# Both products of an MLP as 2x2 block products with seven multiplications, on one Trainium2 core

## The chip, the core and the metric

The kernel runs on one core of one Trainium2 chip. The engines of a core work side by side, each through its own list of instructions in a fixed order: PE (TensorE) multiplies matrices, PEld is its weight load, DVE (VectorE), ACT (ScalarE) and POOL (GpSimd) work element by element, and SP (SyncE) issues the transfers between DRAM and the core's memory. The metric is the device time of one execution in microseconds (us), median of several runs.

## The reference

The program is a stack of three mixing layers of width 1024 over 1024 tokens. The change touches only its end: the norm before the last MLP, the MLP, and the norm behind it. In float32:

```python
    merged = ...                                   # sum of four gated branches, (1, 1024, 1024)
    x = x + rms_norm(merged @ w_out, norm_mix_post)

    h2 = rms_norm(x, norm_mlp_pre)
    u = jax.nn.relu(h2 @ w_mlp_in)                 # w_mlp_in (1024, 4096)
    x = x + rms_norm((u * u) @ w_mlp_out, norm_mlp_post)   # w_mlp_out (4096, 1024)
    return x
```

## The kernel before, in words

Activations lie transposed: a page is 128 features by 512 tokens, so an activation of width 1024 is 8 feature blocks times 2 token halves, 16 pages. A float32 operand is held as two pages or weight tiles, a high part (rounded to the multiplier's format) and a low part (the rest), made by `split` (L101): ACT casts the high part (L104), DVE subtracts it from the source (L105). A product of one weight block of 128x128 with one page is three matmuls of 128x512 in `mm3` (L111): high by high (L113), high by low (L114), low by high (L115).

`merge` (L1755) multiplies the branches by their gates and by `w_out` (`proj`) and ends with `norms`, once for each token half: a row norm (`rnorm`, with small matmuls at L198 and L206 and a power on POOL at L141), the old x from DRAM added (L1803, L1804), x stored to DRAM as `x3`, and a second norm whose 8 results are split into pages `H`.

`mlp` (L1825) then goes over the 4096 inner features in 8 chunks of 4 blocks. `hidden` takes each block: `wload` (L144) fetches 512 KB of weights into `raw` (two buffers) and splits them into `whi` and `wlo` (128x1024), 8 feature blocks by three matmuls give one page per token half, ACT copies it (L1840), DVE applies relu and square in one instruction (L1841), and `split` makes pages `M`. `project` multiplies the 4 blocks of the chunk with the matching rows of `w_mlp_out` for the 8 output blocks and adds the result to 16 accumulators `Y` (L1862). In the first and the last chunk the token halves go one after the other, otherwise together. `finish` is the last norm, for one half under the products of the other.

Counted: each of the two MLP products has 32 x 8 blocks x 2 halves x 3 = 1536 matmuls of 128x512, 3072 in all.

The order of each engine's instructions is set when the program is built, by a scheduler that moves instructions within their data dependences and the free buffers. A tile of a pool can be taken again only when the last reader of its former content is done.

Of the kernel before, what the change touches and what calls it, by code (L numbers as in the profile page):

```python
# [11 lines left out]
F32 = mybir.dt.float32  # L12
F32R = mybir.dt.float32r
BF16 = mybir.dt.bfloat16
AF = mybir.ActivationFunctionType
ALU = mybir.AluOpType
AX = mybir.AxisListType

S = 1024
D = 1024  # L20
P = 128
# [4 lines left out]
N_RAW, N_HI = 2, 2  # L26
NEARLY, NLATE = 4, 8
NS, NL, NN = 32, 7, 5


class Kern:
# [1723 lines left out]
    def merge(self, br):  # L1755
# [41 lines left out]
        def norms(half, ys, acc):  # L1797
            hs = slice(half * 512, half * 512 + 512)
            r = self.rnorm(acc, 1.0 / 1024.0)
            for f in range(8):  # L1800
                xo = self.T("xo", 2)
                nc.sync.dma_start(out=xo, in_=self.x2[f * P:(f + 1) * P, hs])
                nc.vector.scalar_tensor_tensor(out=ys[f], in0=ys[f], scalar=self.n2[:, 8 + f:9 + f], in1=r, op0=ALU.mult, op1=ALU.mult)  # L1803
                nc.vector.tensor_tensor(out=ys[f], in0=ys[f], in1=xo, op=ALU.add)  # L1804
                nc.sync.dma_start(out=self.x3[f * P:(f + 1) * P, hs], in_=ys[f])
            res.append(self.norm_half(ys, self.n2[:, 16:24]))
# [12 lines left out]
        norms(0, ys[0], accs[0])  # L1819
        for f in range(8):  # L1820
            proj(f, 1, ys[1], accs[1])
        norms(1, ys[1], accs[1])
        return self.pair_halves(res)

    def mlp(self, H, out):  # L1825


        nc = self.nc
        FC = 4
        last = 32 // FC - 1  # L1830
        Y = [[None, None] for _ in range(8)]
        def hidden(ch, halves, between=()):
            U = [[None, None] for _ in range(FC)]
            for j in range(FC):
                w = self.wload(self.seg("w_mlp_in", (ch * FC + j) * 1024, 8, 128), 8, 128)
                for half in halves:
                    pt = self.ps("mm")
                    self.fm(pt, w, H, half)
                    t = self.T("M", 32)
                    nc.scalar.copy(t, pt)  # L1840
                    nc.vector.scalar_tensor_tensor(out=t, in0=t, scalar=0.0, in1=t, op0=ALU.max, op1=ALU.mult)  # L1841
                    hi, lo = self.T("M", 32, F32R), self.T("M", 32, F32R)
                    self.split(hi, lo, t)
                    U[j][half] = (hi, lo)
                if between:
                    between[j]()
            return U

        def project(ch, U, halves):
            for dp in range(4):  # L1850
                w = self.wload(self.seg("w_mlp_out", (ch * 4 + dp) * 1024, 4, 256), 4, 256)
                for dd in range(2):
                    d = 2 * dp + dd
                    wd = [(a[:, dd * P:(dd + 1) * P], b[:, dd * P:(dd + 1) * P]) for a, b in w]
                    for half in halves:
                        pt = self.ps("mm")
                        self.fm(pt, wd, U, half)
                        if ch == 0:
                            Y[d][half] = self.T("Y", 16)
                            nc.scalar.copy(Y[d][half], pt)  # L1860
                        else:
                            nc.vector.tensor_tensor(out=Y[d][half], in0=Y[d][half], in1=pt, op=ALU.add)  # L1862

        def olds(half):
            X = [self.T("M", 32) for _ in range(8)]
            for d in range(8):
                nc.sync.dma_start(out=X[d], in_=self.x3[d * P:(d + 1) * P, half * 512:half * 512 + 512])
            return X

        def finish(half, X):  # L1870

            hs = slice(half * 512, half * 512 + 512)
            acc = self.T("yacc", 2)
            for d in range(8):
                self.sumsq_add(acc, Y[d][half], d == 0)
            r = self.rnorm(acc, 1.0 / 1024.0)

            def scale(d0):
                for d in (d0, d0 + 1):
                    y = Y[d][half]  # L1880
                    nc.vector.scalar_tensor_tensor(out=y, in0=y, scalar=self.n2[:, 24 + d:25 + d], in1=r, op0=ALU.mult, op1=ALU.mult)
                    nc.vector.tensor_tensor(out=y, in0=y, in1=X[d], op=ALU.add)
                    nc.sync.dma_start(out=out[d * P:(d + 1) * P, hs], in_=y)
            return [lambda d=d: scale(d) for d in range(0, 8, 2)]

        for ch in range(last):
            for halves in ((0,), (1,)) if ch == 0 else ((0, 1),):
                project(ch, hidden(ch, halves), halves)
        project(last, hidden(last, (0,)), (0,))
        U = hidden(last, (1,), finish(0, olds(0)))  # L1890
        X = olds(1)
        project(last, U, (1,))
        for fn in finish(1, X):
            fn()

    def second_block(self, H, out, end_banks):
# [4 lines left out]
        with tc.tile_pool(name="gp", bufs=1, reuse_waits="tile") as self.gp:  # L1901
# [21 lines left out]
            end_banks()  # L1923
            with self.banks("tail", 4, 0, 1, 2), self.phase("tail"):
                H2 = self.merge(brd)
                self.mlp(H2, out)

# [198 lines left out]
```

## Time and profile before

| | |
|---|---|
| median of 3 runs | 3508.95 us (3502.64 to 3509.22) |
| profiled execution, own time | 3508.32 us |
| its span, first to last instruction | 3506.5 us |
| mean granted TensorE clock in it | 0.984 of full speed |
| PE busy | 3369.9 us (96% of the span) |
| DVE, ACT, POOL busy | 1966.9, 1321.3, 109.2 us |

The profile is one execution. Its span runs from the first to the last instruction; 1.8 us of the measured time lie around it. The part that the change touches is the end of the span, from about 2700 us on: the two `norms` lie between 2720 and 2810 us, the products of the MLP follow, the last of them ends at 3486 us, and the last norm closes the span. A busy time counts an engine as busy while an instruction of it runs. Matmuls overlap one another in the pipeline, so the cost of one is the distance between the starts of two, not its own duration.

### The profile page before, as it was taken

To read this page: it belongs to the slowest core of one execution; us is meant where nothing else is said; L and a number is where in the kernel's file an instruction comes from. 1 tells how busy PE (TensorE), PEld (TensorE's weight loads), DVE (VectorE), ACT (ScalarE), POOL (GpSimd) and SP (SyncE) were. 2 spreads that over 40 slices of the span, in tenths; PEclk is the share of its full clock that TensorE was granted. 3 is DMA by queue.
4 is the path that set the end of the run, shared out by engine and by line. 5 is a ranking of instruction groups with operands and counts; after the bars stand their busy time and mean duration, and the time that the engine had idled before them with its cause. 6 is when DMAs were issued, how large, how long until landed. Compare 5 with 4: busy or idle time off the path is not lost.

```text
span 3506.5 us, 45207 instructions
## 1 busy us (share of the span) xinstructions
PE 3369.9 (96%) x18181; PEld 2812.7 (80%) x18181; DVE 1966.9 (56%) x3418; ACT 1321.3 (38%) x2106; POOL 109.2 (3%) x132
## 2 busy tenths in 40 slices
PE   7999999999999999999999999999989899999997
PEld 5888988777888888787777777779768788888886
DVE  6767644556767644565664367453477743333336
ACT  4656412334655312443312345463233442222222
POOL 0000000000000000000100000000000000000000
PEclk9999999999999999999999999999999999999998
DMA  5111111452111111443231211122275421111114
GB/s 185 57 36 51 50 55 57 140 179 86 48 43 36 41 46 63 158 162 119 87 95 65 67 55 56 49 70 75 85 256 178 158 89 48 48 49 49 49 61 149
DMA packets 138707, 302.34 MB, mean 86 GB/s; under 512 B 23944, under 2 KB 41336, under 8 KB 137984
## 3 DMA queue, kind: packets, MB, share of 16 engines
q1 hardware_dynamic: 129280, 282.65, 24.7%
q10 hardware_dynamic: 9216, 16.78, 1.3%
q8 instruction: 143, 2.34, 0.3%
q14 instruction: 68, 0.56, 0.1%
HBM read 245.30 MB, written 58.28 MB: 87 GB/s over the span
## 4 chain that ended last, share of the span: by engine, by line
PE 83%; DVE 5%; issue 5%; ACT 3%; DMA 3%; POOL 1%; SPq 0%; DVEq 0%; POOLq 0%; ACTq 0%
PE mm L113 21%; PE mm L114 21%; PE mm L115 21%; PE lg L388 2%; PE lg L389 2%; PE tp L512 2%; PE pv L113 1%; PE pv L206 1%; PE pv L114 1%; PE pv L115 1%; DMA S<-mix 1%; PE tp L198 1%; DVE wlo L105 1%; PE tp L1392 1%; ACT whi L104 1%
## 5 line engine op out<-in xcount | busy, mean ns | idle before, releaser
L113 PE MATMUL mm<-H,whi 128*128 128x512 f32 x2400 | 958.2, 400 | 26.9 <-DVE S L369 5.0
L115 PE MATMUL mm<-H,wlo 128*128 128x512 f32 x2400 | 949.4, 396 | 5.9 <-DVE wlo L105 5.7
L114 PE MATMUL mm<-H,whi 128*128 128x512 f32 x2400 | 949.8, 396 | 2.1 <-DVE H L105 2.1
L104 ACT CAST whi<-raw 128x1024 fp32r<-128x1024 f32 (+1 forms) x340 | 334.4, 984 | 860.3 <-PE mm L114 768.7
L105 DVE TENSOR_TENSOR wlo<-raw,whi 128x1024 fp32r<-128x1024 f32 (+1 forms) x340 | 387.4, 1140 | 421.6 <-ACT whi L104 409.9
L113 PEld LDWEIGHTS mm<-H,whi 128*128 128x128 f32 x2400 | 456.5, 190 | 125.5 <-ACT H L107 7.2
L115 PEld LDWEIGHTS mm<-H,wlo 128*128 128x128 f32 x2400 | 455.7, 190 | 104.2 <-DVE wlo L105 12.3
L114 PEld LDWEIGHTS mm<-H,whi 128*128 128x128 f32 x2400 | 456.2, 190 | 92.7 <-DVE H L105 2.9
L113 PE MATMUL mm<-whi,H 128*128 128x256 f32 x960 | 277.2, 289 | 3.9 <-DVE S L576 3.2
L114 PE MATMUL mm<-wlo,H 128*128 128x256 f32 x960 | 274.6, 286 | 3.1 <-DVE wlo L105 3.1
L115 PE MATMUL mm<-whi,H 128*128 128x256 f32 x960 | 273.7, 285 | 0.0
L113 PE MATMUL mm<-M,whi 128*128 128x512 f32 x640 | 249.5, 391 | 1.7 <-ACT whi L104 1.5
L115 PE MATMUL mm<-M,wlo 128*128 128x512 f32 x640 | 249.7, 390 | 0.2 <-DVE wlo L105 0.2
L114 PE MATMUL mm<-M,whi 128*128 128x512 f32 x640 | 249.5, 390 | 0.0
L113 PEld LDWEIGHTS mm<-whi,H 128*128 128x128 f32 x960 | 184.6, 192 | 6.8 <-issue 4.2
L114 PEld LDWEIGHTS mm<-wlo,H 128*128 128x128 f32 x960 | 184.8, 193 | 5.1 <-DVE wlo L105 4.2
L115 PEld LDWEIGHTS mm<-whi,H 128*128 128x128 f32 x960 | 184.6, 192 | 0.4
L489 DVE CUSTOM_DVE_ANT_0 lg<-lg,strip 128x1024 f32<-128x1024 f32 x128 | 155.2, 1234 | 25.8 <-PE lg L389 25.6
L1862 DVE TENSOR_TENSOR Y<-Y,mm 128x512 f32<-128x512 f32 x112 | 77.0, 687 | 159.1 <-PE mm L115 159.0
L493 ACT ACTIVATE L<-lg,mx 128x1024 f32<-128x1024 f32 x128 | 142.7, 1118 | 36.5 <-DVE mx L489 30.3
L113 PEld LDWEIGHTS mm<-M,whi 128*128 128x128 f32 x640 | 120.2, 188 | 28.0 <-ACT whi L104 1.9
L115 PEld LDWEIGHTS mm<-M,wlo 128*128 128x128 f32 x640 | 120.5, 188 | 25.6 <-DVE wlo L105 0.6
(455 smaller groups left out, 4968.0 us busy)
## 6 DMA issues: line engine op xcount, KB each, us to landing
raw<-in_w_in SPq DMA_DIRECT2D x106, 512.0 KB, 3.6
raw<-in_w_out SPq DMA_DIRECT2D x48, 512.0 KB, 4.0
raw<-in_w_gate SPq DMA_DIRECT2D x46, 512.0 KB, 3.5
raw<-in_w_mlp_in SPq DMA_DIRECT2D x40, 512.0 KB, 3.3
raw<-in_w_mlp_out SPq DMA_DIRECT2D x40, 512.0 KB, 3.2
Y<-gates SPq DMA_DIRECT2D x64, 256.0 KB, 5.0
gates<-gs ACTq DMA_DIRECT2D x60, 256.0 KB, 2.0
mix<-S SPq DMA_DIRECT2D x48, 256.0 KB, 2.1
```

Of the source, the lines that this page charges most:

```text
L104: nc.scalar.copy(hi, src)
L105: nc.vector.tensor_tensor(out=lo, in0=src, in1=hi.bitcast(F32), op=ALU.subtract)
L113: mm(out, lh, rh, start=start, stop=False)
L114: mm(out, lh, rl, start=False, stop=False)
L115: mm(out, ll, rh, start=False, stop=stop)
L198: self.nc.tensor.matmul(ss[:, n * i + j:n * i + j + 1], acc[:, j * P:(j + 1) * P], self.one, start=True, stop=True)
L388: mm(out, Q[m][qb // 4][:, sl], KH[m][half][:, o:o + kn], start=True, stop=False)
L389: mm(out, Q[m][qb // 4][:, sl], KL[m][half][:, o:o + kn], start=False, stop=not more)
L489: nc.vector.tensor_tensor_reduce(out=lg, in0=lg, in1=strip[:, w0:w0 + 1024], op0=ALU.add, op1=ALU.min, scale=-1.0, scalar=3.0e38, accum_ou ...
L493: nc.scalar.activation(pm, lg, AF.Exp, bias=mx, scale=-1.0, accum_out=sm)
L512: nc.tensor.transpose(tp[:, j, :], pm[:, kb * P:(kb + 1) * P], self.ident)
L1862: nc.vector.tensor_tensor(out=Y[d][half], in0=Y[d][half], in1=pt, op=ALU.add)
```

## The change

Both MLP products are computed as products of 2x2 blocks with seven block products in place of eight. For one pair of output blocks (2g, 2g+1) the weights are A11, A12 (block 2g, first and second half of the contraction) and A21, A22 (block 2g+1); the activations are B11, B21 (token half 0, first and second half of the contraction) and B12, B22 (token half 1). With

- S1 = A21+A22, S2 = S1-A11, S3 = A11-A21, S4 = A12-S2 (sums of weights, `side_weights`),
- T1 = B12-B11, T2 = B22-T1, T3 = B22-B12, T4 = T2-B21 (sums of pages, `side_sums`),

the seven products are A11 B11, A12 B21, S2 T2, S1 T1, S3 T3, A22 T4 and S4 B22; DVE adds them up to the four results. All the sums S and T are made by POOL. Each S and each T is split into a high and a low part like any operand before.

First product: `norms` now leaves seven sets of four split pages (`keep`) in place of `H`, and its steps for token half 1 are dealt out between the first products. For g = 0 to 7 the two products A11 B11 and A12 B21, which need only half 0, are done ahead in a loop of their own (E = 8); then for g = 0 to 15 the others (five for g below 8, seven from 8 on). After relu and square, the four results of the group go through `side_sums` again, and all seven pages (B11, B21, T2, T1, T3, T4, B22) are written to DRAM.

Second product: the 16 groups of inner pages are contracted in chunks of 3, 3, 3, 3 and 4. For each chunk the seven sets are loaded from DRAM and split (`load`), and four pairs of output blocks are done with seven products of 9 (in the last chunk 12) matmuls. POOL adds three of the intermediate results to the accumulators `Y` (`gather`), DVE the others. In the last chunk half 0 is finished first; S1 T1 and S4 B22, which only half 1 needs, follow in a loop of their own with the weights loaded and summed again, next to the last norm of half 0.

The memory pool of the branch stage is closed before the end stage, which takes 52 tiles of 128x512 that all its pages share.

```diff
+NT = 52
+CHUNKS = [range(0, 3), range(3, 6), range(6, 9), range(9, 12), range(12, 16)]
...
+    def side_sums(self, b11, b21, b12, b22, use):
+        nc = self.nc
+        t1, t2, t3, t4 = (self.T("Y", 16) for _ in range(4))
+        nc.gpsimd.tensor_tensor(out=t1, in0=b12, in1=b11, op=ALU.subtract)
+        nc.gpsimd.tensor_tensor(out=t2, in0=b22, in1=t1, op=ALU.subtract)
+        use("T2", t2)
+        use("T1", t1)
+        nc.gpsimd.tensor_tensor(out=t3, in0=b22, in1=b12, op=ALU.subtract)
+        use("T3", t3)
+        nc.gpsimd.tensor_tensor(out=t4, in0=t2, in1=b21, op=ALU.subtract)
+        use("T4", t4)
+        use("B22", b22)
...
+    def side_weights(self, src1, src2, nb, names):
...
+        for src in (src1, src2):
+            t = self.wp.tile([P, 2 * nb, P], F32, tag="raw", bufs=N_RAW, name=self.nm("raw"))
+            nc.sync.dma_start(out=t, in_=src)
...
+        def sm(a, b, op):
+            t = self.T("ws", 4, F32, (P, nb, P))
+            nc.gpsimd.tensor_tensor(out=t, in0=a, in1=b, op=op)
+            return t
...
+        if "A1" in names:
+            W["A11"], W["A12"] = self.block_weights(raw[0], nb)
+        s1 = sm(a21, a22, ALU.add)
+        s2 = sm(s1, a11, ALU.subtract)
+        part("S2", s2)
+        part("S1", s1)
...
+    def prod(self, w, X):
+        out, n = self.ps("mm"), len(w)
+        for k in range(n):
+            self.mm3(out, w[k][0], w[k][1], X[k][0], X[k][1], k == 0, k == n - 1)
+        return out
...
+        for g in range(NG):
+            names = ("S2", "S1", "S3", "A22", "S4") + (() if g in S1 else ("A1",))
+            W = self.side_weights(wseg(2 * g), wseg(2 * g + 1), 4, names)
...
+            w = add(s1, self.prod(W["S2"], XS["T2"]))
+            if g not in S1:
+                u11 = c11(g, s1, W["A12"])
+            t = add(w, self.prod(W["S1"], XS["T1"]))
+            p7 = self.prod(W["S3"], XS["T3"])
+            add(w, p7, w)
+            u22 = relu2(add(t, p7))
+            u21 = relu2(add(w, self.prod(W["A22"], XS["T4"]), w, ALU.subtract))
+            save(g, "B21", u21)
+            u12 = relu2(add(t, self.prod(W["S4"], XS["B22"]), t))
+            self.side_sums(u11, u21, u12, u22, lambda n, t: save(g, n, t))
...
+        def load(name, gs):
+            res = []
+            for g in gs:
...
+                nc.sync.dma_start(out=lo.bitcast(F32), in_=ud[name][g])
+                nc.scalar.copy(hi, lo.bitcast(F32))
+                nc.vector.tensor_tensor(out=lo, in0=lo.bitcast(F32), in1=hi.bitcast(F32), op=ALU.subtract)
...
+                s1 = copied(self.prod(W["A11"], side("B11")))
+                gather(d1, 0, s1)
+                w = add(s1, self.prod(W["S2"], side("T2")))
+                gather(d1, 1, w)
+                accumulate(d1, 0, self.prod(W["A12"], side("B21")))
+                v = add(w, self.prod(W["S3"], side("T3")))
+                gather(d2, 1, v)
+                gather(d2, 0, v)
...
+            if final:
+                todo = deque(finish(0))
+                for dp in range(4):
...
+                    W = self.side_weights(wseg2(d1), wseg2(d2), nb, ("S1", "S4"))
```

The places where the instructions now stand differently, as the built programs list them:

POOL in the end stage before: it does nothing but the power of the norms (`rn`; the last two belong to `finish`, the others to `norms`).

```order
L141 TENSOR_TENSOR rn_23730<-rn_23730,mhalf 128x4
L141 TENSOR_TENSOR rn_24077<-rn_24077,mhalf 128x4
L141 TENSOR_TENSOR rn_24153<-rn_24153,mhalf 128x4
L141 TENSOR_TENSOR rn_28301<-rn_28301,mhalf 128x4
L141 TENSOR_TENSOR rn_28665<-rn_28665,mhalf 128x4
```

POOL in the changed kernel, first product, from group 0 to group 1: L1890 are sums of weights (S1, S2, S3, S4 of a group), L1861 to L1867 the sums of pages (T1, T2, T3, T4); S_24832 is the page u12 of group 0.

```order
L1890 TENSOR_TENSOR S_24723<-raw_24721 128x512
L1890 TENSOR_TENSOR S_24725<-S_24723,raw_24719 128x512
L1890 TENSOR_TENSOR S_24735<-raw_24719,raw_24721 128x512
L1890 TENSOR_TENSOR S_24745<-raw_24719,S_24725 128x512
L1861 TENSOR_TENSOR S_24834<-S_24832,S_24751 128x512
L1862 TENSOR_TENSOR S_24835<-S_24799,S_24834 128x512
L1865 TENSOR_TENSOR S_24836<-S_24799,S_24832 128x512
L1867 TENSOR_TENSOR S_24837<-S_24835,S_24815 128x512
L1890 TENSOR_TENSOR S_24851<-raw_24849 128x512
L1890 TENSOR_TENSOR S_24853<-S_24851,raw_24847 128x512
L1890 TENSOR_TENSOR S_24863<-raw_24847,raw_24849 128x512
L1890 TENSOR_TENSOR S_24873<-raw_24847,S_24853 128x512
```

The four sums of the weights of group 1 stand behind the four sums of the pages of group 0, and the first of these reads u12.

DVE in the middle of the MLP before: splits of weights (`wlo`), relu (L1841), splits of pages (L105 on `M`) and accumulation (L1862) stand between one another.

```order
L105 TENSOR_TENSOR wlo_27263<-raw_27260,whi_27262 128x1024
L1841 SCALAR_TENSOR_TENSOR M_27191<-M_27191 128x512
L1862 TENSOR_TENSOR Y_24385<-Y_24385,mm_27204 128x512
L105 TENSOR_TENSOR M_27195<-M_27191,M_27194 128x512
L1862 TENSOR_TENSOR Y_24681<-Y_24681,mm_27218 128x512
L1862 TENSOR_TENSOR Y_24400<-Y_24400,mm_27232 128x512
L1862 TENSOR_TENSOR Y_24696<-Y_24696,mm_27246 128x512
L105 TENSOR_TENSOR wlo_27325<-raw_27322,whi_27324 128x1024
```

DVE in the changed kernel, from group 2 to group 3: the last two results of the group (L1950 adds a product in `mm`, L1940 is relu and square), then the five splits of the next group's weights (L110), then the first addition of the next group.

```order
L1950 TENSOR_TENSOR S_25022<-S_25022,mm_25057 128x512
L1940 SCALAR_TENSOR_TENSOR S_25071<-S_25022 128x512
L1950 TENSOR_TENSOR S_25037<-S_25037,mm_25074 128x512
L1940 SCALAR_TENSOR_TENSOR S_25088<-S_25037 128x512
L110 TENSOR_TENSOR S_25112<-S_25109,S_25111 128x512
L110 TENSOR_TENSOR S_25116<-S_25107,S_25115 128x512
L110 TENSOR_TENSOR S_25122<-S_25119,S_25121 128x512
L110 TENSOR_TENSOR S_25126<-raw_25105,S_25125 128x512
L110 TENSOR_TENSOR S_25132<-S_25129,S_25131 128x512
L1950 TENSOR_TENSOR S_25150<-S_24368,mm_25137 128x512
```

All five splits for the next group stand behind relu of the last product of this one.

DVE at the start of the second chunk of the second product in the changed kernel: L2009 makes the low part of a loaded page (`H` and `S`), `mm_27787` is the product S3 T3, `mm_27816` the product S1 T1 that reads the three pages S_27801 to S_27811.

```order
L1950 TENSOR_TENSOR S_27797<-S_27743,mm_27787 128x512
L2009 TENSOR_TENSOR H_28279<-H_28279,H_28280 128x512
L2009 TENSOR_TENSOR S_27801<-S_27801,S_27802 128x512
L2009 TENSOR_TENSOR H_28284<-H_28284,H_28285 128x512
L2009 TENSOR_TENSOR S_27806<-S_27806,S_27807 128x512
L2009 TENSOR_TENSOR H_28289<-H_28289,H_28290 128x512
L2009 TENSOR_TENSOR S_27811<-S_27811,S_27812 128x512
L2009 TENSOR_TENSOR H_28307<-H_28307,H_28308 128x512
L1950 TENSOR_TENSOR S_27196<-S_27196,mm_27816 128x512
```

Between two additions of products stand seven splits of loaded pages, three of this chunk and four of the next.

## Rows read from the trace of the kernel before

**Rows 1.** Page, part 1: engine, busy us, share of the span, instructions.

```profile
PE 3369.9 (96%) x18181; PEld 2812.7 (80%) x18181; DVE 1966.9 (56%) x3418; ACT 1321.3 (38%) x2106; POOL 109.2 (3%) x132
```

**Rows 2.** Windows: stretch, its us, busy us of each engine (instructions), granted clock, DMA, GB/s.

```profile
2820.00:3440.00 620.00, 619.85 (x2734) 512.62 (x2732) 232.32 (x291) 144.65 (x198) 0.00 (x0) 1.00 0.18 60
2706.00:2820.00 114.00, 105.08 (x471) 84.61 (x470) 85.33 (x124) 55.04 (x83) 4.03 (x4) 0.97 0.45 147
```

**Rows 3.** Groups by line and form, 2820 to 3440 us: busy us, mean ns of one.

```profile
L105 DVE TENSOR_TENSOR wlo<-raw,whi 128x1024 fp32r<-128x1024 f32 x66 | 80.9, 1225 | 136.0 <-ACT whi L104 136.0
L1862 DVE TENSOR_TENSOR Y<-Y,mm 128x512 f32<-128x512 f32 x104 | 71.5, 687 | 155.7 <-PE mm L115 155.6
L105 DVE TENSOR_TENSOR M<-M,M 128x512 fp32r<-128x512 f32 x56 | 38.8, 693 | 34.4 <-ACT M L104 34.4
L1841 DVE SCALAR_TENSOR_TENSOR M<-M 128x512 f32<-128x512 f32 x56 | 38.5, 688 | 58.9 <-ACT M L1840 58.9
L104 ACT CAST M<-M 128x512 fp32r<-128x512 f32 x56 | 34.8, 622 | 63.4 <-DVE M L1841 63.4
```

**Rows 4.** Waits of PE from 2690 to 2820 us: total us, times, longest.

```profile
PE mm L113 <- ACT whi L104: 2.6, 2, 1.5
PE tp L198 <- DVE acc L190: 2.2, 2, 1.8
PE pv L206 <- POOL rn L141: 2.1, 3, 0.8
PE mm L115 <- DVE wlo L105: 2.0, 2, 1.8
```

**Rows 5.** Timeline of the end of the last product: start, us, engine, line, instruction.

```profile
3485.75 0.39 PE L115 MATMUL mm<-M,wlo 128*128 128x512 f32 x1
3486.17 0.69 DVE L1862 TENSOR_TENSOR Y<-Y,mm 128x512 f32<-128x512 f32 x1 [0.58 <-PE mm L115]
...
3489.58 0.16 DVE L140 TENSOR_SCALAR rn<-tp 128x4 f32<-128x4 f32 x1 [1.28 <-PE tp L198]
3489.82 1.01 POOL L141 TENSOR_TENSOR rn<-rn,mhalf 128x4 f32<-128x4 f32 x1 [47.16 <-DVE rn L140]
3490.89 2.08 PE L206 MATMUL pv<-c_ident,rn 128*128 128x128 f32 x8 [1.41 <-POOL rn L141]
```

**Rows 6.** Groups of POOL by line and form, whole span.

```profile
L141 POOL TENSOR_TENSOR rn<-rn,mhalf 128x4 f32<-128x4 f32 x34 | 37.3, 1096 | 2098.1 <-DVE rn L140 1536.4 <-DVE smx L494 561.7
L141 POOL TENSOR_TENSOR l<-l,mhalf 128x16 f32<-128x16 f32 x4 | 12.4, 3111 | 141.0 <-DVE l L140 141.0
L362 POOL MEMSET S<- 64x512 f32 x16 | 8.3, 521 | 17.1 <-PE lg L388 6.3 <-DVE N L219 3.3 <-ACT L L104 2.9
L1109 POOL MEMSET BT<- 128x2048 f32 x2 | 3.6, 1804 | 25.4 <-PE lg L1334 25.4
```

**Rows 7.** Timeline of PE around a wait in the second norm.

```profile
2789.08 0.39 PE L114 MATMUL mm<-H,whi 128*128 128x512 f32 x1
2791.28 0.80 PE L115 MATMUL mm<-H,wlo 128*128 128x512 f32 x1 [1.81 <-DVE wlo L105]
2791.88 0.63 PE L113 MATMUL mm<-H,whi 128*128 128x512 f32 x1
2792.30 0.63 PE L114 MATMUL mm<-H,whi 128*128 128x512 f32 x1
...
2794.42 0.39 PE L113 MATMUL mm<-H,whi 128*128 128x512 f32 x1
2794.65 0.40 PE L114 MATMUL mm<-H,whi 128*128 128x512 f32 x1
```

**Rows 8.** DMA issues from 2700 to 2830 us: KB each, median us to landing.

```profile
x<-Y SPq DMA_DIRECT2D x16, 256.0 KB, 3.0
raw<-in_w_mlp_in SPq DMA_DIRECT2D x8, 512.0 KB, 3.3
```

**Rows 9.** Windows: the busiest 10 us of the DMA engines in the end stage.

```profile
2570.00:2580.00 10.00, 9.38 (x40) 7.11 (x39) 8.88 (x13) 7.15 (x12) 0.00 (x0) 1.00 1.03 381
```

More of the change, by code (lines that the diff above doesn't have):

```diff
@@ L28 @@
 NS, NL, NN = 32, 7, 5
+NT = 52
+SETS = ("B11", "B21", "T2", "T1", "T3", "T4", "B22")
+HSETS = ("B11", "B21", "B22")
+HSETS2 = ("B11", "T2", "B21", "T3")
+CHUNKS = [range(0, 3), range(3, 6), range(6, 9), range(9, 12), range(12, 16)]
 class Kern:
@@ L1795, in proj, with norms, first, add @@
             ys.append(y)
-        def norms(half, ys, acc):
+        def norms(half, ys, acc, n2):
             hs = slice(half * 512, half * 512 + 512)
[L1799 to L1806, printed above, removed]
+            st, X = {}, [None] * 8
+            order = [0, 4, 1, 5, 2, 6, 3, 7]
+            def first():
+                st["r"] = self.rnorm(acc, 1.0 / 1024.0)
+                st["acc"] = self.T("acc", 1)
+            def add(fs):
+                for f in fs:
+                    xo = self.T("xo", 2)
+                    nc.sync.dma_start(out=xo, in_=self.x2[f * P:(f + 1) * P, hs])
+                    nc.vector.scalar_tensor_tensor(out=ys[f], in0=ys[f], scalar=self.n2[:, 8 + f:9 + f], in1=st["r"], op0=ALU.mult, op1=ALU.mult)
+                    nc.vector.tensor_tensor(out=ys[f], in0=ys[f], in1=xo, op=ALU.add)
+                    nc.sync.dma_start(out=self.x3[f * P:(f + 1) * P, hs], in_=ys[f])
+                    self.sumsq_add(st["acc"], ys[f], f == 0)
+            def second():
+                st["r2"] = self.rnorm(st["acc"], 1.0 / 1024.0)
+            def scale(fs):
+                for f in fs:
+                    X[f] = self.T("Y", 16)
+                    nc.vector.scalar_tensor_tensor(out=X[f], in0=ys[f], scalar=self.n2[:, 16 + f:17 + f], in1=st["r2"], op0=ALU.mult, op1=ALU.mult)
+                n2(half, fs, X)
+            pairs = [order[2 * i:2 * i + 2] for i in range(4)]
+            return X, [first] + [lambda p=p: add(p) for p in pairs] + [second] + [lambda p=p: scale(p) for p in pairs]
         ys, accs = [[], []], [self.T("yacc", 2) for _ in range(2)]
@@ L1818, in merge @@
             proj(f, 0, ys[0], accs[0])
-        norms(0, ys[0], accs[0])
+        XS = {n: [None] * 4 for n in SETS}
+        X0, steps = norms(0, ys[0], accs[0], lambda half, fs, X: [self.keep(XS, "B11" if f < 4 else "B21", f % 4, X[f]) for f in fs])
+        for fn in steps:
+            fn()
         for f in range(8):
             proj(f, 1, ys[1], accs[1])
-        norms(1, ys[1], accs[1])
-        return self.pair_halves(res)
-    def mlp(self, H, out):
-        nc = self.nc
-        FC = 4
-        last = 32 // FC - 1
-        Y = [[None, None] for _ in range(8)]
[L1832 to L1864, printed above, removed]
@@ new lines, in block_weights @@
+    def block_weights(self, raw, nb):
+        hi = self.wp.tile([P, 2 * nb, P], F32R, tag="whi", bufs=N_HI, name=self.nm("whi"))
+        lo = self.wp.tile([P, 2 * nb, P], F32R, tag="wlo", bufs=N_HI, name=self.nm("wlo"))
+        self.split(hi, lo, raw)
+        w = [(hi[:, k], lo[:, k]) for k in range(2 * nb)]
+        return w[:nb], w[nb:]
+    def prod(self, w, X):
[3 more added lines that the diff above has]
+        return out
@@ L1865, in olds @@
             X = [self.T("M", 32) for _ in range(8)]
             for d in range(8):
[L1867 to L1876, printed above, removed]
+                nc.sync.dma_start(out=X[d], in_=self.x3[d * P:(d + 1) * P, hs])
@@ L1878, in scale, with norm @@
+            st = {}
+            def norm():
+                st["r"] = self.rnorm(accs[half], 1.0 / 1024.0)
             def scale(d0):
@@ L1883, in scale @@
                     nc.sync.dma_start(out=out[d * P:(d + 1) * P, hs], in_=y)
[L1884 to L1894, printed above, removed]
+            return [norm] + [lambda d=d: scale(d) for d in range(0, 8, 2)]
```

144 lines of the change are left out of this document (137 added, 7 removed).

## The prediction

> **What bounds the kernel now.** I read the page's busy times first. PE is busy for 96% of the span, so its work is the bound of the whole [rows 1]; what the change does is decided in the MLP, so the windows come next. From 2820 to 3440 us PE is busy for 619.85 of 620 us at full clock, with 2734 matmuls, one every 0.2268 us, while DVE has 232 us to do, ACT 145 and POOL nothing [rows 2]. So each matmul removed there is worth 0.227 us, and nothing else stands on the path. Only in the two norms in front of it (2706 to 2820 us) does PE lose time, 105 of 114 us busy [rows 2]; the waits that the view lists add up to 8.9 us [rows 4].
>
> The question is whether PE stays fed when POOL makes sums that it didn't make before. The groups by line give the prices of what is added: a DVE instruction on a 128x512 page takes 0.69 us, an ACT cast 0.62, a weight split of 128x1024 on DVE 1.22 [rows 3].
>
> **Removed.** 3072 matmuls become 2688. 384 x 0.2268 = 87.1 us, all on the path.
>
> **Group boundaries of the first product.** This is the term that decides. Each engine keeps its listed order. On POOL the sums of the weights of group g+1 stand behind the page sums of group g, and the first of those reads u12, which comes from the group's last product, S4 B22. PE's next product S2 T2 needs S2, so between two products of PE lies: the rest of the last matmul (0.39 - 0.23 = 0.16), 0.03 to DVE, addition 0.69, relu 0.69, 0.08 to POOL, four page sums and two weight sums on POOL, 0.06 to ACT, cast 0.62, 0.06 to PE [rows 3, 5]. That is 2.39 us plus six times P, P being one POOL sum of 128x512. The third matmul waits for DVE's low part as well (0.69 behind the cast), which the first two hide only at half clock.
>
> The trace has no such sum. Below: POOL writes 512 columns in 0.52 us, and from there to 2048 columns it needs 0.835 ns a column [rows 6]. Above: two reads and a write one after the other, 3 x 0.43, and the fixed share of POOL's two-input power, 1.10 - 4 x 0.168 = 0.42 (0.168 us a column from its 4 and 16 columns) [rows 6]: 1.71. These ends lie far apart; I take the middle, 1.1, because a sum moves more than the memset and its fixed share can hardly exceed the power's. So the chain is 2.39 + 6.6 = 9.0 us. The Trainium skill (GPSIMD Engine Reference, section 3.1) says that a two-input sum costs POOL about 2.6 cycles an element, since both inputs share a read port, and that DVE is about twice as fast. Worked out from the page, that is an estimate of 1.1 to 1.2 us; by the memset row alone the total would be 55 us less, by the page's rate it would be that of my 1.1 or a few us more. No run so far shows which holds.
>
> A wait of this length has a second price. After 3 us with nearly no work PE's matmuls come 0.43 us apart (the lower level, 1.2 GHz) from 2791.3 to 2794.4 us, then 0.23 again [rows 7]: seven matmuls lose 0.2 each, 1.4 us.
>
> What hides the chain: below g = 8 nothing, since the two products that need no sum are done ahead. From g = 8 on A11 B11 of the next group runs first, 12 x 0.2268 = 2.72 us; A12 B21 stands behind the first matmuls of S2 T2 in PE's order and hides nothing. So:
> - into g = 1 to 7: 7 x (9.0 + 1.4) = 73 us
> - into g = 8 to 15: 8 x (9.0 - 2.7 + 1.4) = 62 us
> - into the second product: two of the six sums have 384 columns (0.83): 2.39 + 6.1 - 9 x 0.2268 + 1.4 = 8 us.
>
> Together 143 us, more than the matmuls give back. Each 0.1 us of P moves it by 9.5 us. DVE's order adds nothing to it: the five splits stand behind relu of u12, but S2 is later still. SP is not on this path: the weights of g+1 are issued before the saves of g, need 3.3 us to land [rows 8] and have a whole group for it. The saves, 3.0 us each [rows 8], are behind POOL, and nobody waits for them before the second product.
>
> **The loop ahead of it.** 192 matmuls (43.5 us) cover the second norm, 20 page splits and the relus. DVE has 71 instructions of 0.69 us and 6 weight splits of 1.22 there [rows 3], 56 us. It starts some 3 us after PE and waits twice for the norm's power, about 1.3 us each time [rows 5]. So PE reaches S2 T2 of g = 0 some 56 + 3 + 2.6 - 43.5 = 18 us late. Before, this norm cost about half of the 8.9 us [rows 4]. Cost: +14, bounds 0 and 25.
>
> **Second product.** In the steady state PE has 63 matmuls, 14.3 us, for a pair of blocks, DVE about 8.5 us (7 additions, 5 small splits, one large), POOL 8 sums, 7.7 us: hidden. At the start of a chunk it isn't. Behind the addition of S3 T3, DVE splits seven loaded pages before it adds S1 T1, then three for A22 T4 and three for S4 B22. From the addition on: seven pages 4.9 us, the rest of S1 T1 0.4, its two additions 1.4, three pages 2.1, the rest of A22 T4 and its addition 1.1, three pages 2.1, rest 0.7, in all 12.7. PE's three products are 6.1 us, and A11 B11 of the next pair fills 2.0: 12.7 + 0.7 - 8.1 = 5.3 us late. Thirteen pages and two weight tiles, 4.2 MB, are asked for at that time; at the 381 GB/s that the DMA engines moved at their fullest [rows 9] that is 11 us, just in time. Four chunks make 21 us. The last, with four pages to a set, I put at 8, and 0.8 us of clock at each of the five: 33.
>
> In the loop for S1 and S4 at the end, PE has 5.4 us a pair. POOL's eight sums for the last norm of half 0 stand in front of the next weight sums: from the last product of half 0 to S1 of the second pair lie additions and squares (3 us), the norm (4 us), a scaling 0.7, 8.8 on POOL, one weight sum 1.1 and a cast 0.6, 18 us, of which PE fills 5.4. The two raw buffers are free only when POOL is done with them, so each further pair costs 3.3 us for the sums, and about 5 for 1 MB to land, 8.5 instead of 5.4. Over the 21.8 us of the products that is 13 and, for two further pairs, 6: 19. The closing norm stays as it is.
>
> So +52, bounds 15 (DVE's pages all early, the loop half hidden) and 100 (the transfers late in every chunk).
>
> **Sum.** -87 + 143 + 14 + 52 = +122. The profiled execution took 3508.3 us (span 3506.5 and 1.8 around it), so 3630; the median of the runs is 0.6 us above it, which changes nothing.
>
> **Rivals.**
> - *The sums run ahead.* If POOL's six sums were not between two products, the boundaries would cost only DVE's 2.4 us below g = 8, 17 us in all, and no clock: -87 + 17 + 14 + 52 = -4, 3504 us, no change; with the second product at its lower bound 3467, faster. It decides once the chain is under about 3 us a boundary. For it: PE has 13.6 to 19 us of work in a group and POOL under 9. Against it: POOL's listed order. Chance 0.06.
> - *POOL is cheap*, about the memset's 0.52 us [rows 6]: 122 - 55 = +67, 3575. Chance 0.15.
> - *POOL or the second product is dearer*: P = 1.7 gives another 57, 3687; transfers late in each chunk another 48, 3678. For it: the chunk starts ask for as much as the DMA engines have ever moved here. Chance 0.17.
> - *The clock stays low* for a whole group after each wait, not for 3 us: 53 more matmuls at 0.2 us in 7 groups and 65 in 8, +178, 3808. Against it: the return within 3.1 us [rows 7]. Chance 0.05.
>
> **How the numbers follow.** The forecast, 3600 to 3665 as its own range, has 0.57. The range of 8 in 10 leaves out the rival that runs ahead, the clock, and the outer parts of the two prices of POOL: 3555 to 3715. From no change the measurement of this kernel tells about 0.2%, 7 us. Slower by more than that: 0.93, all cases but the first rival; within it 0.03; faster 0.04.
>
> **What would show it.** In the changed kernel's profile, PE's waits for S2's cast in the first product, 15 of them of 6 to 9 us, and a granted clock at its lower level for some 3 us behind each. POOL's busy time in a group is about 8 x P. In the second product five waits of PE on pages from L2009, and in the last loop waits on POOL. It is wrong if PE runs from group to group without a gap, or if a POOL sum takes under half a microsecond.

## The result, and the profile after

The changed kernel takes 3764.61 us (median of 4 runs, 3757.99 to 3768.15) against 3508.71 (3502.64 to 3509.22): a ratio of 1.0731, 95% interval 1.0712 to 1.0751. It is slower, as forecast, but by 256 us and not by 122, and the time lies 50 us above the range. The profiled execution took 3768.15 us, with a span of 3766.4 us, 260 more than before.

The page's busy times, after [rows 1]: 384 matmuls fewer, but the span grew around them, and POOL's work is five times what it was.

```profile
PE 3383.8 (90%) x17797; PEld 2788.8 (74%) x17797; DVE 2219.2 (59%) x3744; ACT 1377.9 (37%) x2258; POOL 532.4 (14%) x454
```

Windows of the changed kernel: the loop of the merge that makes the gate products of the first half, then the loop ahead of the first product, the first product from S2 of g = 0 on, and the second product [rows 2 for before]. The columns are the stretch, its us, then busy us and instructions of PE, weight loads, DVE, ACT and POOL, the granted clock, DMA share and GB/s.

```profile
2580.00:2660.00 80.00, 54.61 (x190) 42.00 (x190) 53.88 (x79) 17.11 (x23) 0.00 (x0) 0.85 0.59 199
2816.00:2891.00 75.00, 46.68 (x198) 35.69 (x197) 58.16 (x73) 28.45 (x45) 29.28 (x20) 0.87 0.37 128
2891.00:3335.00 444.00, 305.20 (x1162) 240.90 (x1162) 201.08 (x264) 65.05 (x108) 166.36 (x129) 0.82 0.31 110
3335.00:3749.00 414.00, 350.21 (x1354) 268.46 (x1355) 292.88 (x382) 144.70 (x254) 226.29 (x175) 0.87 0.38 127
```

In none of these stretches is an engine full, and the clock is at its lower level for part of each. The first product waits in one way, the second in another; PE's waits (us in total, times, longest), first from 2891 to 3335 us, then from 3335 to 3690 [rows 4 for before]:

```profile
PE mm L118 <- ACT S L109: 155.9, 17, 20.0
PE mm L120 <- DVE S L110: 2.9, 1, 2.9
...
PE mm L119 <- DVE S L2009: 25.7, 18, 2.7
PE mm L119 <- DVE H L2009: 9.2, 9, 2.2
PE mm L118 <- ACT S L109: 9.1, 2, 8.0
PE mm L118 <- ACT H L2008: 4.5, 4, 1.4
PE mm L118 <- ACT S L2008: 2.4, 2, 1.9
```

The wait of 8.0 us is the boundary into the second product; the others stand at the starts of its five chunks and add up to 43 us.

One boundary, from the last product of group 1 to S2 T2 of group 2, in the timeline [rows 5, 7]. It is the chain of the prediction, link for link: addition, relu, four page sums, two weight sums, cast.

```profile
2936.19 0.39 PE L120 MATMUL mm<-H,S 128*128 128x512 f32 x1
2936.62 0.69 DVE L1950 TENSOR_TENSOR S<-S,mm 128x512 f32<-128x512 f32 x1 [1.30 <-PE mm L120]
2937.34 0.69 DVE L1940 SCALAR_TENSOR_TENSOR S<-S 128x512 f32<-128x512 f32 x1
2938.16 1.26 POOL L1861 TENSOR_TENSOR S<-S,S 128x512 f32<-128x512 f32 x1 [16.07 <-DVE S L1940]
...
2943.16 1.26 POOL L1890 TENSOR_TENSOR S<-raw 128x512 f32<-128x512 f32 x1
2945.79 1.85 ACT L109 CAST S<-S 128x512 fp32r<-128x512 f32 x3 [22.45 <-POOL S L1890]
2946.47 0.79 PE L118 MATMUL mm<-S,S 128*128 128x512 f32 x1 [9.89 <-ACT S L109]
...
2952.45 0.59 PE L119 MATMUL mm<-S,S 128*128 128x512 f32 x1
2952.87 0.40 PE L120 MATMUL mm<-S,S 128*128 128x512 f32 x1
```

The matmuls behind it come 0.43 us apart until 2952.9, over 6 us, twice as long as behind the shorter wait of before [rows 7]. That is one of sixteen boundaries, with waits of 7.2 to 10.0 us; behind them this lasts from 3.0 to 6.4 us, and costs 2.4 us in the mean.

POOL's groups from 2891 to 3335 us (busy us, mean ns of one), the price that no row of before had [rows 6]:

```profile
L1861 POOL TENSOR_TENSOR S<-S,S 128x512 f32<-128x512 f32 x16 | 20.4, 1274 | 271.3 <-DVE S L1940 252.2 <-PE mm L120 19.1
L1890 POOL TENSOR_TENSOR S<-raw 128x512 f32<-128x512 f32 x15 | 18.9, 1262 | 0.0
```

**Where the 260 us are.** I measured stretches between the same matmuls in both traces (a stretch's loss is its length less 0.2268 us for each matmul of 128x512 in it).

| Stretch | forecast | measured |
|---|---|---|
| 384 matmuls fewer | -87 | -87 |
| up to the merge, where nothing is changed | 0 | +6 |
| merge, up to the first matmul of the MLP (206.1, now 236.6 us) | not named | +30 |
| loop ahead of the first product (loss 10.7, now 37.4) | +14 | +27 |
| first product (444.1 us for 1161 matmuls) | +143 | +181 |
| second product and closing norm (loss 26.1, now 128.7) | +52 | +103 |

The 6 us are within what executions of one kernel differ by (3502.64 to 3509.22). Of the 103 us, 79 are lost at the five chunk starts, between the same matmuls (12, 16, 18, 18 and 15 us), where the forecast had 33; the last loop with the closing norm loses 50, where before the end lost 26, so 24 more against a forecast of 19. Of the 79, 43 are the waits above, 10 the slower step from one matmul to the next right at a wait, and 26 matmuls between the waits that come more than 0.2268 us apart; the granted clock of the five starts is 0.66 to 0.80.

### The profile page after: what moved, and what is told of

It is laid out like the page before. It is cut to its first block, busy times and chain, and to the rows that moved or that the text cites. A ratio compares the mean times of both kernels' runs of the same rounds, so it can differ in the third digit from the quotient of the medians.

```text
span 3766.4 us, 46285 instructions
## 1 busy us (share of the span) xinstructions
PE 3383.8 (90%) x17797; PEld 2788.8 (74%) x17797; DVE 2219.2 (59%) x3744; ACT 1377.9 (37%) x2258; POOL 532.4 (14%) x454
## 4 chain that ended last, share of the span: by engine, by line
PE 74%; issue 7%; DVE 7%; POOL 5%; ACT 4%; DMA 3%; SPq 1%; POOLq 0%; DVEq 0%; ACTq 0%
PE mm L118 19%; PE mm L119 19%; PE mm L120 19%; PE lg L393 2%; POOL S L1890 2%; PE lg L394 2%; PE tp L517 1%; DMA S<-mix 1%; DVE wlo L110 1%; ACT whi L109 1%; PE pv L118 1%; PE pv L119 1%; PE pv L211 1%; PE pv L120 1%; PE tp L1397 1%
## 5 line engine op out<-in xcount | busy, mean ns | idle before, releaser
L118 PE MATMUL mm<-H,whi 128*128 128x512 f32 x2144 | 868.5, 405 | 54.2 <-DVE S L1785 17.4
L119 PE MATMUL mm<-H,whi 128*128 128x512 f32 x2144 | 858.6, 401 | 4.8 <-DVE H L2009 4.8
L120 PE MATMUL mm<-H,wlo 128*128 128x512 f32 x2144 | 856.6, 400 | 4.9 <-DVE wlo L110 4.6
L118 PEld LDWEIGHTS mm<-H,whi 128*128 128x128 f32 x2144 | 414.4, 193 | 148.3 <-issue 22.1
L110 DVE TENSOR_TENSOR wlo<-raw,whi 128x1024 fp32r<-128x1024 f32 (+4 forms) x296 | 330.7, 1118 | 322.3 <-ACT whi L109 311.7
L109 ACT CAST whi<-raw 128x1024 fp32r<-128x1024 f32 (+4 forms) x296 | 284.3, 962 | 545.1 <-PE mm L119 407.3
L119 PEld LDWEIGHTS mm<-H,whi 128*128 128x128 f32 x2144 | 413.6, 193 | 88.9 <-DVE H L2009 6.4
L118 PE MATMUL mm<-S,S 128*128 128x512 f32 x448 | 198.7, 444 | 159.9 <-ACT S L109 147.9
L109 ACT CAST S<-S 128x512 fp32r<-128x512 f32 (+1 forms) x200 | 113.3, 584 | 548.3 <-POOL S L1890 463.9
L110 DVE TENSOR_TENSOR S<-S,S 128x512 fp32r<-128x512 f32 (+1 forms) x200 | 175.2, 898 | 199.7 <-ACT S L109 199.7
L1950 DVE TENSOR_TENSOR S<-S,mm 128x512 f32<-128x512 f32 x252 | 168.8, 683 | 174.0 <-PE mm L120 151.7
L118 PEld LDWEIGHTS mm<-S,S 128*128 128x128 f32 x448 | 96.1, 214 | 189.9 <-ACT S L109 154.6
L119 PE MATMUL mm<-S,S 128*128 128x512 f32 x448 | 197.0, 440 | 29.4 <-DVE S L2009 29.2
L120 PE MATMUL mm<-S,S 128*128 128x512 f32 x448 | 193.2, 431 | 3.7 <-DVE S L110 3.7
```

What stands on the lines that cost most here:

```text
L109: nc.scalar.copy(hi, src)
L110: nc.vector.tensor_tensor(out=lo, in0=src, in1=hi.bitcast(F32), op=ALU.subtract)
L118: mm(out, lh, rh, start=start, stop=False)
L119: mm(out, lh, rl, start=False, stop=False)
L120: mm(out, ll, rh, start=False, stop=stop)
L1950: nc.vector.tensor_tensor(out=out, in0=a, in1=ps, op=op)
```

## The experiments

Line numbers of the runs' rows shift by a few against the changed kernel.

**One: DVE's order in the merge.** The diff doesn't touch the loop that makes the gate products, and yet it lost 28 us (52.3 us before, 80.6 now). The scheduler listed it anew, presumably since the tiles come from a common pool now (that this is the reason wasn't tried). On DVE, the weight split of round f+2 stands ahead of the reads of round f's products; one round of the changed kernel:

```profile
2611.41 1.04 ACT L109 CAST whi<-raw 128x1024 fp32r<-128x1024 f32 x1 [2.93 <-PE mm L119]
2612.48 1.22 DVE L110 TENSOR_TENSOR wlo<-raw,whi 128x1024 fp32r<-128x1024 f32 x1 [3.28 <-ACT whi L109]
2613.63 1.88 DVE L1785 SCALAR_TENSOR_TENSOR S<-S,mm 128x512 f32<-128x512 f32 x3
2614.45 0.47 PE L118 MATMUL mm<-H,whi 128*128 128x512 f32 x1 [2.90 <-DVE S L1785]
```

The split needs the cast, the cast needs the buffer that PE reads until the end of round f, and behind the split stand the reads that empty the four PSUM banks PE needs for round f+1. So nothing overlaps. The edit puts the split behind the reads:

```diff
 w = self.wload(self.seg("w_up", f * 1024, 8, 128), 8, 128)
+if len(done) > 1:   # done[-2]: last gate product of two rounds before
+    tc.add_manual_dep(split_of(w), done[-2].ins.name, NoSync)
```

> Only DVE's order in the loop that makes the gate products of the merge is put back to that of the kernel before (the split of the weights of round f+2 again behind the gate products of round f, by an edge that orders the two on DVE); the MLP is untouched. Theory 1 (one instruction at the head of DVE's list holds back the reads of four full PSUM banks): the seven waits of 2.9 to 3.3 us there and the clock dips behind them go, 7 x (3.1 + 0.9) = 28 us, 3737 us. Theory 2 (the loop is late because its pages and gates come from DRAM through fewer free tiles): the waits stay under another name, 3755 to 3770 us.

It took 3745.15 us (3740.0 to 3757.72), 19 less. PE's waits in the loop, first of the changed kernel, 2580 to 2661 us, then of this run, 2569 to 2630:

```profile
PE mm L118 <- DVE S L1785: 17.4, 6, 2.9
PE mm L118 <- ACT H L109: 7.7, 1, 7.7
...
PE mm L118 <- ACT H L109: 8.6, 1, 8.6
PE mm L118 <- ACT whi L109: 5.1, 5, 1.0
PE mm L118 <- DVE S L1787: 1.4, 1, 1.4
```

The 17.4 us on L1785 are 1.4 now, and the loop takes 60.9 us. Theory 1 holds for 20 of its 28 us. The loop is still 8.6 us longer than before: 4.8 of that is the wait for the pages of the second half (8.6 us; 3.7 before, 7.7 in the changed kernel), most of the rest are the five waits for weight casts, which have come in place of those on L1785. What makes the long one longer wasn't tried.

**Two: the weight sums listed ahead of the page sums.**

```diff
+if g + 1 < NG:
+    nxt = self.side_weights(wseg(2 * g + 2), wseg(2 * g + 3), 4, ...)
 self.side_sums(u11, u21, u12, u22, ...)
```

> The sums of the weights of group g+1 are made ahead of the page sums of group g; same instructions, same engines. Theory 1 (the boundary is a chain of listed work on POOL): of the 9.9 us only DVE's addition, relu and the split of S2 are left, 0.16 + 0.03 + 3 x 0.69 = 2.3 us less the two matmuls that need no low part, some 1.8 us below g = 8 and nothing from g = 8 on, where A11 B11 covers it. 7 x 8.1 + 8 x 7.3 = 115 us and most of the 37 us of low clock behind the waits: 3615 to 3650 us. Theory 2 (POOL and DVE hold each other up, so the work takes as long wherever it is listed): under half of that, 3700 us or more.

It took 3636.87 us, 128 less, with the same instructions on the same engines. The first product went from 444.1 to 314.5 us. From g = 9 on there is no wait above 0.3 us until the boundary into the second product, which keeps 9.6 us; at most of the earlier boundaries 0.7 to 4 us are left, and they have another cause. POOL, in the run's timeline:

```profile
2977.38 1.30 POOL L1867 TENSOR_TENSOR S<-S,S 128x512 f32<-128x512 f32 x1
2984.02 1.26 POOL L1890 TENSOR_TENSOR S<-raw 128x512 f32<-128x512 f32 x1 [5.34 <-DMA raw<-in_w_mlp_in]
```

POOL is free early and waits for the weights, whose load SP issues behind the saves of pages. The boundary was a chain of listed order; behind it stood the next wait.

**Three: PE kept busy at the boundaries**, with products that nobody reads.

```diff
+for i in range(14 if g in S1 else 10):
+    self.mm3(pt, *W0["S4"][i % 4], *XS["B22"][i % 4], True, True)
 w = add(s1, self.prod(W["S2"], XS["T2"]))
```

> PE gets 42 matmuls at each boundary into g = 1 to 7 and 30 at each from g = 8 on, of loaded weights and pages, whose result is not used; nothing else changes, so S2 arrives as late as before. Theory 1 (the slow matmuls behind a boundary come from PE having been idle): the clock stays at its upper level and 15 x 2.4 = 37 us come back, 3728 us. Theory 2 (they are slow for another reason, such as weights that come late): 3760 us or more.

It took 3735.3 us, 29 less, though S2 comes as late as before. The end of the added matmuls and the start of S2 T2:

```profile
2932.64 0.39 PE L120 MATMUL mm<-H,S 128*128 128x512 f32 x1
2933.57 0.50 PE L118 MATMUL mm<-S,S 128*128 128x512 f32 x1 [0.54 <-ACT S L109]
2934.70 0.50 PE L120 MATMUL mm<-S,S 128*128 128x512 f32 x1 [0.39 <-DVE S L110]
2935.03 0.40 PE L118 MATMUL mm<-S,S 128*128 128x512 f32 x1
```

But for the one short wait in these rows, the matmuls behind the boundary are at most 0.34 us apart from the first on, and 0.23 from the fifth. A group takes 24.65 us instead of 26.3 below g = 8 and 27.35 instead of 28.8 above, 7 x 1.65 + 8 x 1.45 = 23 of the 29 us. Idleness ahead of them is what made them slow.

**Four: the weight sums on DVE.** One word of the code: `nc.gpsimd` becomes `nc.vector` in the function that sums two weight blocks.

> All sums of weights, of both products, are made by DVE instead of POOL; the page sums and the gathers stay on POOL. Theory 1 (the chain as it was counted): page sums leave the chain and two sums cost 0.69 each, 0.16 + 0.03 + 4 x 0.69 + 0.06 + 0.62 + 0.06 = 3.7 us instead of 9.9, so 7 x 6.2 + 8 x 6.3 = 94 us and about 20 us of clock: 3650 us, the second product the same within 15 us. Theory 2 (DVE's instructions with two SBUF inputs run at half speed while POOL sums, 1.48 us instead of 0.69): with POOL's share halved the second product gains another 30 us or more, 3620 us or less.

It took 3659.33 us, near theory 1 (3650). The boundary waits are 4.5 us where 3.7 were counted, the first product 343.0 us; the second gained 6 us, not 30: its chunk starts lose 68 us instead of 79, but the last loop and the norm 55 instead of 50. The 0.8 us have a row: DVE's sums come in two prices, 1.63 us where POOL's page sums run beside them, 0.68 where they don't.

```profile
L1890 DVE TENSOR_TENSOR S<-raw,raw 128x512 f32<-128x512 f32 x16 | 26.1, 1629 | 0.0
...
L1890 DVE TENSOR_TENSOR S<-raw,S 128x512 f32<-128x512 f32 x16 | 10.9, 684 | 0.0
```

**Five and six: the second product without POOL's work, and without the splits.** In the first, a block stands for each weight sum and the later gathers are left out; in the second the loaded page serves as both parts.

```diff
+if not sums: return a                 # five, second product only
-nc.gpsimd.tensor_tensor(out=Y[d][half], in0=Y[d][half], in1=t, op=ALU.add)
---
-nc.scalar.copy(hi, lo); nc.vector.tensor_tensor(out=lo, in0=lo, in1=hi, ...)   # six
-res.append((hi, lo))
+res.append((lo, lo))
```

> POOL has nothing to do in the second product: blocks of the loaded weights stand for their sums and the 64 gathers after the first are left out, so its result is incomplete; everything else is as in the changed kernel. Theory 1 (at the chunk starts DVE's splits run at half speed beside POOL, 1.48 us instead of 0.69): the splits take 0.69 again, the chunk starts fall from 83 us of waits and low clock to about the 33 that were forecast, and the last loop loses its 8.8 us wait: 3700 to 3715 us. Theory 2 (the pages come late from DRAM): PE's waits stay, now for pages, 3745 us or more.

> The pages of the second product are used as they are loaded, as high and as low part; ACT and DVE don't split them, so the result is inexact. Theory 1 (the split pages are DVE's work at the start of a chunk): nearly all of the 83 us of the chunk starts goes, 3680 to 3700 us. Theory 2 (the transfers are late): at most a third of it goes, 3740 us or more.

Five took 3714.66 us, 50 less, six 3685.39, 79 less. DVE's split of a loaded page in the second product, first of the changed kernel:

```profile
L1950 DVE TENSOR_TENSOR S<-S,mm 128x512 f32<-128x512 f32 x126 | 84.1, 681 | 57.6 <-PE mm L120 47.4 <-POOL S L2022 7.7 <-POOL S L2020 2.4
L2009 DVE TENSOR_TENSOR H<-H,H 128x512 fp32r<-128x512 f32 x52 | 52.2, 1011 | 6.4 <-ACT H L2008 6.2
L2009 DVE TENSOR_TENSOR S<-S,S 128x512 fp32r<-128x512 f32 x40 | 39.0, 1016 | 0.0
```

then of run five:

```profile
L1952 DVE TENSOR_TENSOR S<-S,mm 128x512 f32<-128x512 f32 x127 | 85.6, 685 | 66.1 <-PE mm L120 65.1 <-POOL S L2022 0.7
L2011 DVE TENSOR_TENSOR H<-H,H 128x512 fp32r<-128x512 f32 x53 | 36.3, 691 | 10.0 <-ACT H L2010 9.8
L2011 DVE TENSOR_TENSOR S<-S,S 128x512 fp32r<-128x512 f32 x40 | 25.8, 686 | 0.0
```

Without POOL beside it a split takes 0.69 us, the price that I forecast; with it, 1.01 in the mean. The addition that reads PSUM takes 0.68 in both: only instructions with two inputs in SBUF are held up. In run six PE's waits in the second product, 3329 to 3610 us, are nearly gone, with the same pages loaded at the same places:

```profile
PE mm L118 <- ACT S L109: 8.4, 2, 7.2
PE mm L118 <- DMA S<-uT: 0.8, 1, 0.8
PE mm L120 <- DVE S L110: 0.4, 1, 0.4
```

(7.2 of it is the boundary into the product.) So at the chunk starts the transfers are in time, and what PE waits for there is DVE's splits. Between the same matmuls as above, the five chunk starts lose 79 us in the changed kernel, 41 in run five and 6 in run six; the waits in them are 43 us in the changed kernel and 21 in run five, the slow matmuls between the waits 26 and 15. The last loop with the closing norm hardly changes (50, 49 and 46 us): other waits come in place of those that go, in run six one of 6.1 us for a page that is still on its way from DRAM. Of the 50 us of run five, 6 are the boundary into the second product, which needs no sum any more. Run five takes away POOL's work as a whole, not only its interference: DVE's 7.7 us of waits for gathers (first row) go with it.

The price of a split can also be told apart inside the changed kernel's own trace. Of its 112 splits on L2009, the 56 that met no instruction of POOL took 0.68 us in the mean and at most 0.69; the 37 that had POOL at work for over nine tenths of their time took 1.40 in the mean and up to 1.78. The additions that read PSUM took 0.68 us in either case.

**Seven: both edits of one and two.**

> Both edits that helped: the weight sums of the next group ahead of the page sums, and DVE's order in the merge loop put back. Theory 1 (two separate places): the gains add, 128 + 20 us, 3617 us. Theory 2 (what the merge loop gains is lost in the norm behind it, which then waits longer): 3630 us or more.

3621.62 us, 15 less than two alone: the gains add, within what runs differ by.

**Eight to ten: the first product by seven, the second by eight.** Four sets of pages are saved and loaded a chunk ahead; behind the first norm POOL makes weight sums only.

```diff
-self.side_sums(u11, u21, u12, u22, lambda n, t: save(g, n, t))
+save(g, "B12", u12)     # and u11, u21, u22
...
+pt = self.prod(w1 + w2, U[ci][n1] + U[ci][n2])   # 8 pages, 24 matmuls
```

> The first product by seven block products with both edits of the run before; the second by eight, from the four sets of pages in DRAM, in four chunks of four groups loaded a chunk ahead; no page sums and no gathers behind the first norm. Theory 1 (the second product by seven costs more than the 44 us of matmuls that it saves): second product 1536 x 0.2268 = 348 us with some 15 us of waits, first product 290 us, about 3545 us. Theory 2 (its price was only the boundary into it, and it pays): 3617 us or more. Below 3507 us it would beat both kernels, for which the boundaries of the first product would have to cost nothing.

3531.67 us, ratio 1.0061 (1.0041 to 1.0081), better than theory 1. Then nine, with the weights of the next group listed before the group's last two products, and ten, with E = 12 for 8:

> As the run with only the first product by seven, but the weights of group g+1 are listed ahead of the last two products of group g (so DVE splits S2 before it adds and squares u12), and the first chunk of the second product loads into the tiles that the pages of the merge leave. Theory 1 (the 1.4 us that PE waits at each of seven boundaries are DVE's listed order): the boundaries go, 7 x 1.8 = 12 us, and some 5 of the 8 at the start of the second product: 3514 us. Theory 2 (the weights land late, behind the saves): the wait comes back as one on the cast, 3525 us or more.

> The same, with the two products that need no sum done ahead for twelve groups instead of eight, 4 x 24 x 0.2268 = 21.8 us more under the norm of the second half, where PE waits 21 + 3 us for S2 of the first group. Theory 1 (that wait is DVE's and POOL's work, which goes on beside PE): 3514 - 20 = 3494 us, faster than the kernel before. Theory 2 (the added weight splits and relus on DVE push the sums back by what PE gains): 3505 us or more.

Nine took 3511.68 us (ratio 1.0012, 1.0003 to 1.0021), ten 3501.71 us (0.9984, 0.9975 to 0.9992). In nine the boundaries are gone. In ten PE's wait of 18.3 us for S2 of group 0 became 1.0; the median fell by 10 us of the 20 expected, since part of it came back in the loop ahead: its short waits on ACT's casts and copies and on DVE are 7 us longer in total.

**Eleven: both products by seven, listed as in nine.**

> Both products by seven, as changed, with DVE's order in the merge put back and the weights of group g+1 listed ahead of the last two products of group g (the T4 pages of the merge stand in other tiles, to make room). Theory 1 (order is all that the first product loses): its 51 us above the matmuls, of which 30 are boundaries, fall to some 15, 3621 - 35 = 3586 us; what is left to the version with the second product by eight and the same eight groups ahead, 3512 us, some 75 us, is the price of the second product by seven. Theory 2 (eight POOL sums a group, 10 to 12 us beside 13.6 us of products, and DVE's splits slowed by them are a bound of their own): 3605 us or more.

3598.23 us, between the theories. The first product, 1152 matmuls from S2 T2 of group 0 on, takes 275.6 us, against 266.9 in nine, where POOL has no page sums; the second, with the closing norm, 453.7 against 376.7. So the second product by seven, as it is built here, costs 77 us in the end, though it has 192 matmuls (43.5 us) fewer. Nine differs in its chunks too (four of four groups, loaded a chunk ahead), and that wasn't tried apart.

**Twelve: the norm of the first half listed between the merge's last products**, on top of ten.

```diff
-for fn in steps: fn()
+steps = deque(steps)
 for f in range(8):
     proj(f, 1, ys[1], accs[1])
+    for _ in range(2 if f in (0, 4) else 1): steps.popleft()()
```

> As the run with twelve groups ahead, with the norm of the first half listed between the last eight products of the merge, not in front of them, so that the weight split that PE waits 6.0 us for no longer stands behind the norm on DVE. Theory 1: that wait and the two short ones behind it go, 3502 - 7 = 3495 us. Theory 2 (the norm of half 0 then ends later, and the loop of the products that need no sum waits for its pages): 3502 us or more.

3493.83 us (3489.67 to 3499.02), ratio 0.9967 (0.9954 to 0.998): 12 us faster than the kernel before. Its merge takes as long as before (200 us for 768 matmuls in both), so the gain is the first product's. Its first and second product, and the longest of PE's waits in them:

```profile
2871.00:3118.00 247.00, 244.94 (x1079) 202.48 (x1080) 168.82 (x248) 59.31 (x98) 84.70 (x62) 1.00 0.41 140
3118.00:3465.00 347.00, 344.29 (x1523) 283.94 (x1522) 131.65 (x163) 88.29 (x125) 14.45 (x9) 1.00 0.34 114
...
PE mm L120 <- DVE S L110: 1.8, 1, 1.8
PE mm L118 <- ACT H L2011: 1.2, 1, 1.2
```

PE is full again, as in rows 2, and here a removed matmul is worth its 0.2268 us. The 192 removed are worth 43.5 us; the MLP as a whole gives 25 of them back (in the profiled executions it loses 62 us where it lost 37), 22 of these in the loop ahead.

## Why the prediction was right about the sign and wrong about the size

- *Removed, -87.* Right.
- *Group boundaries, +143.* The chain was right, link by link. The term was too small by 38 us, in three sizes. P was 1.27 and not 1.1: six sums make 1.0 us a boundary, 16 us over the sixteen. The estimate worked out from the Trainium skill (GPSIMD Engine Reference, section 3.1), 1.1 to 1.2 us, is below the measured 1.26 to 1.27 as well, if nearer than my 1.1; the ratio of about two that the page gives agrees, 1.27 to 0.68. The clock costs 2.4 us a boundary and not 1.4, 16 us: I took the 3.1 us behind one wait of 1.8 us as the rule, and behind these waits the matmuls stayed slow for 3.0 to 6.4 us. And group 0 lost 5 us that I hadn't counted.
- *The loop ahead, +14.* It is 27, a little above its upper bound of 25. The wait for S2 is 20 us where 18 were worked out. But PE also waits six times for casts of weights, 7.7 us in all, for which the sum had no term: it had DVE busy for 56 us and idle for some 6, and DVE was busy for 60 of 81 us and idle for 21.
- *Second product, +52.* This step failed: its 103 us lie above my upper bound of 100. The step said that DVE splits seven pages in 4.9 us and is 5.3 us late at a chunk start, with 0.8 us of clock, 33 us for the five starts. The place and the releaser were right; two sizes were not, and the five starts cost 79. One is the price of a split. I took 0.69 from a trace in which POOL did nothing, and never asked what it is beside the sums that the same change gives to POOL: 1.01 in the mean. The waits, with the slow step at each, are 53 us where 29 were forecast, and 25 in run five, where the price is 0.69. The other is the clock. I put down 4 us for the five starts; the matmuls stayed slow between the short waits, 4 to 6 us at each start and 26 in all, and still 15 in run five. My upper bound had transfers late in every chunk as the danger, which run six rules out.
- *The merge, not in the sum.* This was the plainest miss: 30 us, 28 of them in a loop whose code isn't in the diff. I compared the listed order for the MLP and not for the merge, though the pool of tiles, which the scheduler goes by, changed for both. Run one shows 20 of them as DVE's order.
- *Rivals.* "The sums run ahead" was tried in run two: the boundaries shrink as the rival said, but weights that land late keep some. Its price of 3504 us was wrong all the same: with the boundaries gone in run eleven the kernel takes 3598, since its sum had the same terms for the loop ahead and the second product, and nothing for the merge. "The clock stays low for a whole group" is refuted: it returned within 6.4 us. "POOL or the second product is dearer" is what happened, but not as it was priced: P was 1.27 and not 1.7, which is 16 us and not 57, and the second product was 51 us dearer, about the 48 put down for late transfers, by splits and clock, with the transfers in time at the chunk starts. That these two numbers are close is luck.

The sum of the forecast's own misses is 6 + 30 + 13 + 38 + 51 = 138 us, all that were missing. Left open: the 8.6 us wait in the merge, why slow matmuls behind waits of nearly one length last 3 us in some cases and 6 in others, and how much of the second product's 26 us of clock would be left if the splits alone were cheaper, since run five took away POOL's work as a whole.

## What to carry to other kernels

A change that gives work to an idle engine can change the prices on another one, as POOL's sums did with DVE's splits (0.69 to 1.01 us): be wary of a duration from a trace in which that neighbour slept. When a change alters what the scheduler sees (pools, tiles, buffer counts), compare the listed order of every loop in that scope, not only of those in the diff. And before dropping a product that saves too little, try its halves: here the first product by seven, with its weights listed early and the merge back at its former length, was worth 12 us, and the second, as built, cost 77.

## What the hardware showed that I had not expected

- DVE and POOL. A DVE instruction with two inputs in SBUF took 0.69 us alone and up to 1.78 us beside POOL's sums, 1.48 in the rows below; POOL's weight sums of 128x512 took 1.26 us at the least and up to 1.8. In a chunk start of the changed kernel the two alternate:

```profile
3492.60 1.44 POOL L1890 TENSOR_TENSOR S<-raw 128x384 f32<-128x384 f32 x1
3493.11 1.48 DVE L2009 TENSOR_TENSOR S<-S,S 128x512 fp32r<-128x512 f32 x1
3494.12 1.33 POOL L1890 TENSOR_TENSOR S<-S,raw 128x384 f32<-128x384 f32 x1
3494.51 1.49 DVE L2009 TENSOR_TENSOR H<-H,H 128x512 fp32r<-128x512 f32 x1
```

  The Trainium skill (SBUF — State Buffer, section "Who interferes with whom") says that a DVE instruction with two SBUF inputs contends with a GpSimd instruction that reads SBUF, and one with at most one SBUF input, outside the two-port modes, doesn't; rows and rule agree: the split with two SBUF inputs takes 1.01 us in the mean with POOL at work and 0.69 without, the addition that reads PSUM 0.68 in both.
- The clock. Behind the sixteen waits of 7 to 10 us at the boundaries the matmuls came at the lower level for 3.0 to 6.4 us, behind one of 1.8 us for 3.1 [rows 7], so the length of the wait alone doesn't tell how long it lasts. Between the short waits at a chunk start, none over 2.7 us, it cost 4 to 6 us. With PE kept busy through the boundary (run three) the matmuls didn't slow, and the added ones cost nothing, since PE had nothing else to do.
